# Scores of the first token block in a block-attention layer: one TensorE matmul over the keys' high and low parts side by side, and a VectorE add

## The chip, the cores and the metric

The kernel runs on one core of a Trainium2 chip. The metric is the device time of one execution in microseconds (us), taken as the median of several runs. Five engines matter: TensorE (PE in the rows, its weight loads PEld), VectorE (DVE), ScalarE (ACT), GpSimd (POOL) and the queue that issues the transfers (SP).

## What is computed

One attention layer of a decoder, 256 tokens of 1024 channels, 16 heads of 64, and a final RMSNorm. With 256 tokens and blocks of 256 keys there is only the token's own block, so the attention is causal softmax with a linear distance penalty:

```python
h = rms_norm(x, norm_g)
q, k, v, gate = split(h @ w_in, 4)                   # 1024 x 4096
s = (q . k) * 64**-0.5 - slope[head] * (t - pos)     # -inf where pos > t
o = softmax(s) @ v                                   # per head
x = x + (o * silu(gate)) @ w_out
out = rms_norm(x, final_norm_g)
```

All is float32. The kernel reaches that accuracy by splitting each operand into a high part (rounded to the matmul's input format) and a low part (the rest), and summing three products: high by high, high by low, low by high.

## The kernel before, in words

The 256 tokens are two token blocks of 128 (`m = 0`, `m = 1`). Heads are handled in eight pairs `p`: a pair's q and k lie transposed on the 128 partitions, 64 for each of its two heads (`a = 0, 1`), 256 tokens wide.

The body of the kernel is a long stream of TensorE matmuls for the input projection (column parts in the order of `PARTS`: v, q, k, gate and so on) and then for the output projection (`outmm`, one weight piece per `k`; for the last four `k` one output column group after the other). Each weight piece of 128 x 1024 is loaded by a transfer, rounded by ScalarE (`split_hi`, tile `whi`) and subtracted by VectorE (`split_lo`, tile `wlo`, line 251). The attention of each pair is a Python generator, a fiber, whose steps are emitted between the projection's matmuls. A planner (`Plan`) keeps a running estimate of TensorE's position and of the backlog of ScalarE and VectorE; a fiber's next step is emitted when the planned TensorE time has reached the time at which its input is planned to be ready (`yield`, `poll`, `until`). The result is one fixed order of instructions for each engine; the chip then works each engine's list in order.

A pair's steps are:

- `fiber_evac` multiplies a projection's PSUM bank by the row scale into `z` (line 497), ScalarE rounds it to the high part and VectorE subtracts (line 510) for the low part. The two parts of q and of k are two tiles each.
- `scores(p)`, called for an even `p`, does pairs `p` and `p + 1` together, in four PSUM banks, one for each head. For `m = 1` each head has a result of 128 x 256 in columns 0 to 255 of its bank; for `m = 0` the causal part is only 128 x 128, in columns 256 to 383. For each there are three matmuls, and the two heads of a pair work on different halves of the rows at the same time. There are four such score stages.
- `fiber_pair` then has VectorE add the bias (distance penalty and mask) to each result, read from PSUM, with the row's minimum of the negative as a by-product (line 380), ScalarE the exponential with the row sum, VectorE the reciprocal and the scaling (lines 390 to 403), TensorE the transposes of `pr` (line 111), ScalarE and VectorE their split (`pth`, `ptl`, line 426), TensorE the product with the values, ScalarE a copy (`cs`), VectorE two adds (`og`, line 458), the gate (line 462), ScalarE the rounding (`oh`) and VectorE the rest (`ol`, line 467). `oh` and `ol` of pair `p` are the operands of the output projection's piece `k = p`.

The score bank goes back to the pool after the `m = 0` step of its head (`give(bs[a], d)`).

Of the kernel before, what the change touches and what calls it, by code (L numbers as in the profile page):

```python
# [9 lines left out]
F32R = mybir.dt.float32r  # L10
# [3 lines left out]
P = 128  # L14
S = 256
# [72 lines left out]
def trunk(ctx: ExitStack, tc, laid, fin_g, out):  # L88
    nc = tc.nc
    plan = Plan()  # L90
# [32 lines left out]
    def dve(n, dep, rate=0.96, extra=0):  # L123
        return plan.op("dve", 66 + extra + n / rate, dep)
# [166 lines left out]
    qs, ks = {}, {}  # L291
# [32 lines left out]
    def scores(p):  # L324


        while not all(u in at_k and u in at_q for u in (p, p + 1)):
            yield poll()
        yield max(t[u] for t in (at_k, at_q) for u in (p, p + 1))
        while stage["s"] < p:  # L330
            yield poll()
        while True:
            b0 = take(keep[0] + 3)
            if b0 is not None:
                break
            yield poll()
        both = [b0] + [take_now() for _ in range(3)]
        plan.pe += SWITCH
        for u in (p, p + 1):
            of_pair[u] = both[2 * (u - p):2 * (u - p) + 2], {}  # L340
        for m, c in ((1, slice(0, S)), (0, slice(S, S + P))):
            for u in (p, p + 1):
                bs, at_s = of_pair[u]
                (qh, ql), (kh, kl) = qs[u], ks[u]
                for jj, (q, k) in enumerate(((qh, kh), (qh, kl), (ql, kh))):
                    for a in range(2):
                        rr = slice(a * DH, (a + 1) * DH)
                        nc.tensor.matmul(bs[a]["t"][:, c], q[rr, m * P:(m + 1) * P], k[rr, 0:c.stop - c.start],  # L348
                                         start=jj == 0, stop=jj == 2)
                    at_s[m] = plan.mm(c.stop - c.start)  # L350
        plan.pe += SWITCH
        stage["s"] = p + 2
        yield 0

    def fiber_pair(p):
        if p % 2 == 0:
            yield from scores(p)
        while stage["s"] <= p:
            yield poll()
        bs, at_s = of_pair.pop(p)  # L360
        while stage["t"] < p - NPR + 1:
            yield poll()
        st = sp.tile([P, 2, P + S], F32, name="st")
        pr = sp.tile([P, 2, P + S], F32, name="pr")
        mx = sm.tile([P, 4], F32, name="mx")
        rs = sm.tile([P, 4], F32, name="rs")
        ri = sm.tile([P, 4], F32, name="ri")
        r = at_s[0]
        yield 0
        for m in (1, 0):  # L370
            n = (m + 1) * P
            for a in range(2):
                yield r - 250
                while plan.t["act"] > plan.pe + BACK or plan.t["dve"] > plan.pe + BACK:
                    yield poll()
                c0, c1 = (0, P) if m == 0 else (P, P + S)
                bt = bias[:, 2 * p + a, P:S] if m == 0 else bias[:, 2 * p + a, :]
                cc = 2 * m + a
                ps = bs[a]["t"][:, 0:S] if m else bs[a]["t"][:, S:S + P]
                nc.vector.tensor_tensor_reduce(st[:, a, c0:c1], ps, bt, scale=-1.0, scalar=BIG,  # L380
                                               op0=ALU.add, op1=ALU.min, accum_out=mx[:, cc:cc + 1])
                d = dve(n, r, extra=8)
                yield d - 150
                e = act(pr[:, a, c0:c1], st[:, a, c0:c1], AF.Exp, n, d, False, scale=-1.0, bias=mx[:, cc:cc + 1],
                        accum=rs[:, cc:cc + 1])
                if m == 0:
                    give(bs[a], d)
        stage["e"] += 1
        yield e - 400
        nc.vector.tensor_scalar(rs, rs, 2.0, None, op0=ALU.mult)  # L390
        dve(4, e)
        yield plan.t["dve"] - 50
        nc.vector.reciprocal(ri, rs)
        d = d_ri = dve(4, e, extra=157)
        for a in range(2):
            for m in range(NM):
                c0, c1 = (0, P) if m == 0 else (P, P + S)
                cc = 2 * m + a
                o = pr[:, a, c0:c1]
                if plan.t["act"] + NORM < plan.t["dve"]:  # L400
                    d = max(d, act(o, o, AF.Copy, c1 - c0, d_ri, False, scale=ri[:, cc:cc + 1]))
                else:
                    nc.vector.tensor_scalar(o, o, ri[:, cc:cc + 1], None, op0=ALU.mult)
                    d = max(d, dve(c1 - c0, 0, rate=1.92, extra=62))
        d0 = d
        yield d0
        while stage["t"] < p or stage["v"] < p - NPT + 1:
            yield poll()
        hi = ptp.tile([P, 2, 3, P], F32R, name="pth")
        lo = ptp.tile([P, 2, 3, P], F32R, name="ptl")  # L410
        for a in range(2):
            while True:
                b = take(keep[0])
                if b is not None:
                    break
                yield poll()
            for jj in range(3):
                r = tr(b["t"][:, jj * P:(jj + 1) * P], pr[:, a, jj * P:(jj + 1) * P], d0)
                if a == 1 and jj == 2:
                    stage["t"] = p + 1  # L420
                yield 0
            pv = b["t"][:, :3 * P].rearrange("p (a n) -> p a n", a=3)
            yield r - 200
            e = act(hi[:, a], pv, AF.Copy, 3 * P, r, True)
            yield e - 200
            nc.vector.tensor_sub(lo[:, a], pv, f32(hi[:, a]))  # L426
            d = dve(3 * P, e)
            give(b, d)
        while nv[p // 4] < NM:
            yield poll()  # L430
        yield max(d, at_v[p // 4])
        while stage["v"] < p or p not in at_g:
            yield poll()
        while True:
            b = take(keep[0])
            if b is not None:
                break
            yield poll()
        po = b["t"].rearrange("p (a n) -> p a n", a=2)

        for a in range(2):
            w = [vv[m][:, 2 * p + a].rearrange("p t n -> p (t n)") for m in range(NM)]
            for jj, u in enumerate((hi, lo)):
                mm(po[:, a, :], w[0], u[:, a, 0:2, :], jj == 0, False, S)
            yield 0
            for jj, u in enumerate((hi, lo)):
                r = mm(po[:, a, P:S], w[1], u[:, a, 2, :], False, jj == 1, P)
            if a == 1:
                stage["v"] = p + 1
            yield 0  # L450
        yield r - 300
        cs = csp.tile([DH, 2, S], F32, name="cs")
        e = act(cs, po[DH:P], AF.Copy, 2 * S, r, True)
        yield e - 200
        og = ogp.tile([P, S], F32, name="og")
        for a in range(2):
            rr = slice(a * DH, (a + 1) * DH)
            nc.vector.tensor_add(og[rr, :], po[0:DH, a, :], cs[:, a, :])  # L458
            d = dve(S, e)
        give(b, d)  # L460
        yield max(d, at_g[p]) - 200
        nc.vector.tensor_mul(og, og, sg[:, p, :])
        d = dve(S, max(d, at_g[p]))
        yield d - 200
        e = act(oh[:, p, :], og, AF.Copy, S, d, False)
        yield e - 200
        nc.vector.tensor_sub(ol[:, p, :], og, f32(oh[:, p, :]))
        at_o[p] = dve(S, e)
# [6 lines left out]
    def fiber_evac(kind, j, f, b, r):  # L475
        ps = b["t"][:, :S]
        p = 2 * j + f
# [25 lines left out]
        yield d - 100  # L503
        if kind != "g":
            pool = qp if kind == "q" else khp
            hi = pool.tile([P, S], F32R, name=f"{kind}h")
            lo = pool.tile([P, S], F32R, name=f"{kind}l")
            e = act(hi, z, AF.Copy, S, d, False)
            yield e - 100
            nc.vector.tensor_sub(lo, z, f32(hi))  # L510
            (qs if kind == "q" else ks)[p] = (hi, lo)
            (at_q if kind == "q" else at_k)[p] = dve(S, e)
        else:
            e = act(sg[:, p, :], z, AF.Tanh, S, d, False, scale=0.5)
            yield e - 100
            nc.vector.scalar_tensor_tensor(sg[:, p, :], sg[:, p, :], 1.0, z, op0=ALU.add, op1=ALU.mult)
            at_g[p] = dve(S, e)

    with tc.manual_schedule():
# [132 lines left out]
        for kind, j in PARTS[1:]:  # L652
# [4 lines left out]
            for k in range(NK):  # L657
# [5 lines left out]
                for f in range(2):  # L663
                    fs = slice(f * P, (f + 1) * P)
                    for jj, (xx, ww) in enumerate(((xh, whi), (xl, whi), (xh, wlo))):
                        if kind == "v":
                            o, a, b = acc[f]["t"], xx[k][:, fs], ww[i][:, kk * w:(kk + 1) * w]
                        else:
                            o, a, b = acc[f]["t"][:, :S], ww[i][:, kk * w + f * P:kk * w + (f + 1) * P], xx[k]
# [33 lines left out]
        for m in range(NM):  # L703
# [4 lines left out]
            for u, (c0, c1) in enumerate(GROUPS[m]):  # L708
                c = slice(c0, c1)
# [63 lines left out]
```

## Time and profile before

| what | value |
|---|---|
| median of 3 runs | 146.40 us (146.39 to 146.41) |
| profiled execution | 146.18 us, of which the span from the first to the last instruction is 144.4 us |
| TensorE busy | 137.2 us (95% of the span), 1009 matmuls |
| VectorE busy | 119.5 us (83%), 291 instructions |
| ScalarE busy | 92.1 us (64%), 197 instructions |
| granted TensorE clock, mean | 0.99 of full speed |

A row of a timeline gives start, duration, engine, line, operation, output and inputs, the number of instructions merged, and in brackets how long the engine stood idle before it and what released it. Matmuls are pipelined: the row's duration of a matmul holds its latency, and its cost to the stream is read from start to start. "x2" at a score matmul is the two heads of a pair, which start together.

### The profile page before, as it was taken

Reading aid. Unit: us, or ns where it says so; the run is one execution under the profiler, and the core shown is the slowest. Engines: PE = TensorE matmul, PEld = TensorE weight load, DVE = VectorE, ACT = ScalarE, POOL = GpSimd, SP = SyncE. Lnnn points to the kernel's source line nnn. Section 1 sums busy time; section 2 is a strip of 40 time slices with the busy share of each in tenths; the row PEclk is TensorE's granted clock in tenths of the full one; section 3 lists DMA queues with packets and bytes.
Section 4 is the critical chain, followed back from the end, with each engine's and each line's share of the span. In section 5 each row is a group of like instructions: output and inputs, shape, how many; then the busy total and the mean of one; then the engine's idle time right before and its main releaser. Section 6 shows DMA issues by size and latency. Waiting matters only on the chain.

```text
span 144.4 us, 2760 instructions
## 1 busy us (share of the span) xinstructions
PE 137.2 (95%) x1009; PEld 126.0 (87%) x1009; DVE 119.5 (83%) x291; ACT 92.1 (64%) x197; POOL 13.6 (9%) x29
## 2 busy tenths in 40 slices
PE   7999999999999999999999999999999999999930
PEld 5588999999999999999988889999999888868830
DVE  0999399978877999999899699886869996975870
ACT  3698979657779476967293987426595855812330
POOL 7891140000000000000000000000000000000210
PEclk9999999999999999999999999999999999999995
DMA  5999998687015147454536215566614044000123
GB/s 150 350 393 409 414 405 320 201 291 257 22 49 188 58 145 232 137 178 180 194 110 205 82 47 184 204 241 215 239 42 150 0 145 145 0 0 5 39 108 145
DMA packets 8078, 24.83 MB, mean 172 GB/s; under 512 B 896, under 2 KB 1408, under 8 KB 8064
## 3 DMA queue, kind: packets, MB, share of 16 engines
q1 hardware_dynamic: 7632, 23.73, 46.3%
q10 hardware_dynamic: 432, 0.92, 1.7%
q8 instruction: 8, 0.13, 0.4%
q14 instruction: 6, 0.05, 0.1%
HBM read 23.60 MB, written 1.05 MB: 171 GB/s over the span
## 4 chain that ended last, share of the span: by engine, by line
PE 84%; issue 4%; ACT 3%; DVE 3%; DMA 2%; POOL 1%; POOLq 0%
PE bank L107 76%; PE bank L348 4%; PE bank L111 4%; DMA w<-in_laid 2%; ACT whi L118 1%; DVE xl L251 1%; ACT xh L118 1%; POOL fr L726 1%; DVE og L458 1%; DVE bias L717 1%; ACT oh L118 1%; ACT bias L728 1%; POOLq L769 0%; DVE x L715 0%; ACT cs L118 0%
## 5 line engine op out<-in xcount | busy, mean ns | idle before, releaser
L107 PE MATMUL bank<-xh,wlo 128*128 128x256 f32 x192 | 55.2, 288 | 0.0
L107 PE MATMUL bank<-xl,whi 128*128 128x256 f32 x192 | 55.2, 288 | 0.0
L107 PE MATMUL bank<-xh,whi 128*128 128x256 f32 x192 | 55.0, 287 | 0.0
L251 DVE TENSOR_TENSOR wlo<-w,whi 128x1024 fp32r<-128x1024 f32 (+1 forms) x43 | 48.8, 1141 | 6.6 <-ACT whi L118 6.6
L118 ACT ACTIVATE whi<-w 128x1024 fp32r<-128x1024 f32 (+1 forms) x43 | 41.9, 976 | 14.3 <-PE bank L107 7.6
L107 PEld LDWEIGHTS bank<-xl,whi 128*128 128x128 f32 x192 | 36.2, 189 | 0.2
L107 PEld LDWEIGHTS bank<-xh,wlo 128*128 128x128 f32 x192 | 36.2, 189 | 0.2
L107 PEld LDWEIGHTS bank<-xh,whi 128*128 128x128 f32 x192 | 36.2, 189 | 0.1
L118 ACT ACTIVATE pr<-st,mx 128x256 f32<-128x256 f32 (+1 forms) x32 | 14.2, 444 | 7.4 <-DVE mx L380 7.4
L107 PE MATMUL bank<-whi,ol 128*128 128x512 f32 (+1 forms) x35 | 12.8, 364 | 0.0
L726 POOL TENSOR_TENSOR fr<-fms,mhalf 128x1 f32<-128x1 f32 x2 | 1.6, 797 | 117.8 <-DVE fms L717 117.8
L107 PE MATMUL bank<-whi,oh 128*128 128x512 f32 (+1 forms) x35 | 12.6, 361 | 0.0
L107 PE MATMUL bank<-wlo,oh 128*128 128x512 f32 (+1 forms) x35 | 12.6, 359 | 0.0
L111 PE MATMUL bank<-ident,pr 128*128 128x128 f32 x48 | 12.1, 272 | 0.0
L107 PE MATMUL bank<-whi,xh 128*128 128x512 f32 x32 | 11.7, 407 | 0.2 <-ACT whi L118 0.2
L107 PE MATMUL bank<-wlo,xh 128*128 128x512 f32 x32 | 11.6, 403 | 0.0
L107 PE MATMUL bank<-whi,xl 128*128 128x512 f32 x32 | 11.5, 398 | 0.0
L497 DVE TENSOR_TENSOR z<-bank,rows 128x256 f32<-128x256 f32 x24 | 9.5, 419 | 2.3 <-PE bank L107 2.3
L380 DVE CUSTOM_DVE_ANT_0 st<-bank,bias 128x256 f32<-128x256 f32 (+1 forms) x32 | 9.8, 350 | 0.3 <-PE bank L348 0.3
L118 ACT ACTIVATE pth<-bank 128x384 fp32r<-128x384 f32 x16 | 7.8, 489 | 2.7 <-PE bank L111 2.4
L426 DVE TENSOR_TENSOR ptl<-bank,pth 128x384 fp32r<-128x384 f32 x16 | 8.6, 551 | 0.5 <-ACT pth L118 0.5
L107 PE MATMUL bank<-ptl,vv 128*128 128x256 f32 (+1 forms) x32 | 8.9, 279 | 0.0
(81 smaller groups left out, 209.8 us busy)
## 6 DMA issues: line engine op xcount, KB each, us to landing
w<-in_laid SPq DMA_DIRECT2D x36, 512.0 KB, 3.5
w<-in_laid SPq DMA_DIRECT2D x7, 256.0 KB, 4.9
x<-in_laid SPq DMA_DIRECT2D x2, 512.0 KB, 6.8
head<-in_laid SPq DMA_DIRECT2D x3, 256.0 KB, 5.1
out<-bias SPq DMA_DIRECT2D x2, 320.0 KB, 2.3
gf<-in_fin_g ACTq DMA_DIRECT2D x1, 512.0 KB, 5.5
out<-bias SPq DMA_DIRECT2D x2, 192.0 KB, 1.9
w<-in_laid ACTq DMA_DIRECT2D x1, 256.0 KB, 3.1
```

The lines of the kernel that those rows point to most:

```text
L107: nc.tensor.matmul(o, a, b, start=start, stop=stop)
L111: nc.tensor.transpose(o, a, ident)
L118: nc.scalar.activation(o, i, fn, scale=scale, **kw)
L251: nc.vector.tensor_sub(wlo[i][:, c], w32[i][:, c], f32(whi[i][:, c]))
L348: nc.tensor.matmul(bs[a]["t"][:, c], q[rr, m * P:(m + 1) * P], k[rr, 0:c.stop - c.start], start=jj == 0, stop=jj == 2)
L380: nc.vector.tensor_tensor_reduce(st[:, a, c0:c1], ps, bt, scale=-1.0, scalar=BIG, op0=ALU.add, op1=ALU.min, accum_out=mx[:, cc:cc + 1])
L426: nc.vector.tensor_sub(lo[:, a], pv, f32(hi[:, a]))
L458: nc.vector.tensor_add(og[rr, :], po[0:DH, a, :], cs[:, a, :])
L497: nc.vector.tensor_mul(z, ps, rows8 if kind == "q" else rows)
L717: nc.vector.tensor_tensor_reduce(sq[:, :c1 - c0], y[:, c], y[:, c], scale=1.0 / D, scalar=ms[:, u - 1:u], op0=ALU.mult, op1=ALU.add, accum ...
L726: nc.gpsimd.tensor_tensor(r, ms[:, ns - 1:ns], mhalf, op=ALU.pow)
L728: nc.scalar.activation(z[:, 0:CW], z[:, 0:CW], AF.Copy, scale=r)
```

## The change

For `m = 0` the three matmuls per head become two. The first has the high part of q as stationary operand and the high and the low part of k side by side as moving operand (2 x 128 columns); its result is 128 x 256, the high-by-high product in columns 256 to 383 and the high-by-low product in columns 384 to 511 of the head's bank. The second adds low q by high k to the first half. The two halves are added afterwards: VectorE adds the second half and the bias into `st`, and the instruction of line 380 takes `st` in place of the bias. For this the two parts of k (and of q) become two halves of one tile. `m = 1` keeps its three matmuls. The planner is told of the two matmuls (`plan.mm(n * len(ts))`) and of the add (`dve(n, r)`).

```diff
-                (qh, ql), (kh, kl) = qs[u], ks[u]
-                for jj, (q, k) in enumerate(((qh, kh), (qh, kl), (ql, kh))):
+                (qh, ql), kt = qs[u], ks[u]
+                n = c.stop - c.start
+                terms = ((qh, (0, 1)), (ql, (0,))) if m == 0 else ((qh, (0,)), (qh, (1,)), (ql, (0,)))
+                for jj, (q, ts) in enumerate(terms):
                     for a in range(2):
                         rr = slice(a * DH, (a + 1) * DH)
-                        nc.tensor.matmul(bs[a]["t"][:, c], q[rr, m * P:(m + 1) * P], k[rr, 0:c.stop - c.start],
-                                         start=jj == 0, stop=jj == 2)
-                    at_s[m] = plan.mm(c.stop - c.start)
+                        o = bs[a]["t"][:, c.start:c.start + n * len(ts)]
+                        o = o.rearrange("p (t n) -> p t n", n=n)
+                        nc.tensor.matmul(o, q[rr, m * P:(m + 1) * P], kt[rr, ts[0]:ts[-1] + 1, 0:n],
+                                         start=jj == 0, stop=jj == len(terms) - 1, skip_group_check=True)
+                    at_s[m] = plan.mm(n * len(ts))
@@
+                if m == 0:
+                    nc.vector.tensor_add(st[:, a, c0:c1], bs[a]["t"][:, S + P:S + 2 * P], bt)
+                    bt = st[:, a, c0:c1]
+                    dve(n, r)
                 nc.vector.tensor_tensor_reduce(st[:, a, c0:c1], ps, bt, scale=-1.0, scalar=BIG,
                                                op0=ALU.add, op1=ALU.min, accum_out=mx[:, cc:cc + 1])
@@
-            hi = pool.tile([P, S], F32R, name=f"{kind}h")
-            lo = pool.tile([P, S], F32R, name=f"{kind}l")
+            both = pool.tile([P, 2, S], F32R, name=kind)
+            hi, lo = both[:, 0], both[:, 1]
@@
-            (qs if kind == "q" else ks)[p] = (hi, lo)
+            (qs if kind == "q" else ks)[p] = (hi, lo) if kind == "q" else both
```

## Rows read from the trace of the kernel before

**Rows 1.** The page: busy time of the engines, share of the span, instructions.
```profile
PE 137.2 (95%) x1009; PEld 126.0 (87%) x1009; DVE 119.5 (83%) x291; ACT 92.1 (64%) x197; POOL 13.6 (9%) x29
```

**Rows 2.** The two longest waits of the weight loads of the projections (columns: who waited for whom, us in total, times, longest).
```profile
PEld bank L107 <- ACT whi L118: 0.9, 1, 0.9
PEld bank L107 <- ACT oh L118: 0.6, 1, 0.6
```

**Rows 3.** The chain of work that ended last, in order of time: the first and the last of the four score stages on it, which have the same length (start, us, engine, line, matmuls).
```profile
31.80 1.53 PE bank L348 x24
...
101.12 1.53 PE bank L348 x24
```

**Rows 4.** TensorE's timeline around the first score stage: the last step of `m = 1`, the first three and the last of the six steps of `m = 0`, and the projection's matmul that follows.
```profile
32.42 0.30 PE L348 MATMUL bank<-kh,ql 64*128 64x256 f32 x2
32.54 0.24 PE L348 MATMUL bank<-kh,qh 64*128 64x128 f32 x2
32.60 0.29 PE L348 MATMUL bank<-kl,qh 64*128 64x128 f32 x2
32.71 0.29 PE L348 MATMUL bank<-kh,ql 64*128 64x128 f32 x2
...
33.05 0.29 PE L348 MATMUL bank<-kh,ql 64*128 64x128 f32 x2
33.27 0.38 PE L107 MATMUL bank<-xh,wlo 128*128 128x256 f32 x1
```

**Rows 5.** Two of the weight loads of the same steps.
```profile
32.65 0.21 PEld L348 LDWEIGHTS bank<-kh,ql 64*128 64x128 f32 x2
32.76 0.21 PEld L348 LDWEIGHTS bank<-kh,qh 64*128 64x128 f32 x2
```

**Rows 6.** VectorE's groups by line and shape (instructions, busy us, mean ns of one): adds from PSUM of 256 and 384 columns, and the bias step of 128 columns.
```profile
L497 DVE TENSOR_TENSOR z<-bank,rows 128x256 f32<-128x256 f32 x24 | 9.5, 419 | 2.3 <-PE bank L107 2.3
L426 DVE TENSOR_TENSOR ptl<-bank,pth 128x384 fp32r<-128x384 f32 x16 | 8.6, 551 | 0.5 <-ACT pth L118 0.5
L380 DVE CUSTOM_DVE_ANT_0 st<-bank,bias 128x128 f32<-128x128 f32 x16 | 4.4, 282 | 0.0
```

**Rows 7.** VectorE's timeline after the last score stage, with the first (103.87) and the last (109.89) of its four bias steps of `m = 0`, and each instruction ahead of which VectorE stood idle for over 0.2 us.
```profile
103.87 0.29 DVE L380 CUSTOM_DVE_ANT_0 st<-bank,bias 128x128 f32<-128x128 f32 x1
...
104.54 0.42 DVE L497 TENSOR_TENSOR z<-bank,rows 128x256 f32<-128x256 f32 x1 [0.37 <-PE bank L107]
...
106.46 0.43 DVE L516 SCALAR_TENSOR_TENSOR head<-head,z 128x256 f32<-128x256 f32 x1 [0.27 <-ACT head L118]
107.79 1.23 DVE L251 TENSOR_TENSOR wlo<-w,whi 128x1024 fp32r<-128x1024 f32 x1 [0.91 <-ACT whi L118]
...
109.89 0.28 DVE L380 CUSTOM_DVE_ANT_0 st<-bank,bias 128x128 f32<-128x128 f32 x1
```

**Rows 8.** Two dependent instructions of VectorE, one behind the other, for pair 2 (reciprocal, scaling of `pr`).
```profile
60.34 0.18 DVE L393 RECIPROCAL ri<-rs 128x4 f32<-128x4 f32 x1
60.56 1.01 DVE L403 TENSOR_SCALAR pr<-pr,ri 128x128 f32<-128x128 f32 x4
```

**Rows 9.** Busy time of each engine (PE, PEld, DVE, ACT, POOL, each with its instructions; then the granted clock, the transfers' share and GB/s) in four stretches: score stages 1 and 2, each with what follows up to the first transposes of its pairs, stage 4 with what follows it, and the stretch behind that.
```profile
31.70:41.10 9.40, 9.40 (x91) 9.30 (x91) 7.78 (x32) 6.57 (x23) 0.00 (x0) 1.00 0.40 137
53.00:62.50 9.50, 9.50 (x93) 9.43 (x92) 9.16 (x32) 6.96 (x21) 0.00 (x0) 1.00 0.52 167
101.00:107.80 6.80, 6.80 (x69) 6.68 (x69) 4.84 (x20) 5.13 (x18) 0.00 (x0) 1.00 0.40 149
107.80:121.70 13.90, 13.90 (x96) 12.51 (x96) 12.74 (x32) 9.27 (x17) 0.00 (x0) 1.00 0.34 112
```

**Rows 10.** VectorE's timeline in the last part of the kernel: the splits of the transposes of the last two pairs, and what stands around them.
```profile
116.92 1.05 DVE L426 TENSOR_TENSOR ptl<-bank,pth 128x384 fp32r<-128x384 f32 x2
...
119.49 1.21 DVE L251 TENSOR_TENSOR wlo<-w,whi 128x1024 fp32r<-128x1024 f32 x1
121.76 0.85 DVE L458 TENSOR_TENSOR og<-bank,cs 64x256 f32<-64x256 f32 x2 [1.06 <-ACT cs L118]
122.64 0.56 DVE L426 TENSOR_TENSOR ptl<-bank,pth 128x384 fp32r<-128x384 f32 x1
```

**Rows 11.** TensorE's timeline: the first transpose of pair 2, the first matmul with the values for pair 6 (119.37) and for pair 7 (123.44), and the place where the output projection comes to piece 7.
```profile
62.18 0.27 PE L111 MATMUL bank<-ident,pr 128*128 128x128 f32 x1
...
119.37 0.28 PE L107 MATMUL bank<-pth,vv 128*128 128x256 f32 x1
...
123.44 0.28 PE L107 MATMUL bank<-pth,vv 128*128 128x256 f32 x1
...
128.59 0.39 PE L107 MATMUL bank<-whi,ol 128*128 128x512 f32 x1
129.13 0.50 PE L107 MATMUL bank<-xh,oh 128*128 128x512 f32 x1
```

**Rows 12.** The chain of work that ended last, its part from the values of pair 7 to piece 7 of the output projection.
```profile
125.57 0.60 ACT cs L118
...
127.07 1.23 DVE xl L251
128.66 0.43 ACT oh L118
...
129.13 3.77 PE bank L107 x15
```

## The prediction

> **What bounds the kernel now.** I began with the busy times: TensorE is busy for 95% of the span and VectorE for 83% [rows 1]. An average does not say which of them sets the end, so next I read who waited for whom. The longest waits of the projections' weight loads are one for ScalarE's `whi`, 0.9 us, and one for `oh`, 0.6 us [rows 2]; the first is that for the first pieces of the kernel, the second the one that the chain at the end goes through. From the first score stage to 128.59 us no other engine made a hole in TensorE's list. So there TensorE's own work sets the time, and a microsecond taken out of it is a microsecond, as long as the other engines keep up with a TensorE that runs earlier. The chain that ended last agrees: it runs along TensorE, all four score stages lie on it, of 1.53 us each [rows 3], and it leaves TensorE only near the end, for the last pair's `cs`, `og`, gate and `oh` [rows 12]. There TensorE stands: from 128.59 to 129.13 is 0.54 us start to start, where 15 matmuls took 3.77 us, 0.25 each, so about 0.29 us is waiting [rows 11, 12].
>
> So there are two questions: how much shorter a score stage gets, and whether VectorE, which gets more work, falls behind far enough to be met at the end.
>
> **TensorE's part.** The steps of `m = 0` have only 128 moving columns, and yet one follows another at 0.11 us: 32.60 to 32.71, and 32.60 to 33.05 for four steps, which is 0.1125 each. A step of `m = 1`, of 256 columns, takes 0.12 (32.42 to 32.54) [rows 4]. So halving the columns saves almost nothing. The weight loads of these steps stand at the same distance, 32.65 to 32.76 [rows 5]: every step brings a new stationary operand, and that sets the pace. The change replaces three loads per pair by two. Three steps of 0.11 become one of 0.12 and one of 0.11: 0.33 less 0.23 is 0.10 us for each pair, two pairs in a stage, four stages: 8 x 0.10 = 0.80 us. Bounds: the shortest distance in the rows is 0.06 (32.54 to 32.60, behind a 256-column step whose length hides a load) [rows 4]. If the dropped step were worth only that, 8 x (0.06 - 0.01) = 0.40 us; if it were worth a 256-column step, 8 x 0.12 = 0.96. I take 0.80, since four of the five distances between these steps are of that kind. That the two heads of a pair work side by side, and the 0.22 us from the last score step to the next projection matmul (33.05 to 33.27) [rows 4], stay as they are. The moving operand is now two runs of 128 columns with a gap of 128 between them. No row shows such an operand at full clock; I price it at nothing within the bound above, because the result is still one run of 256.
>
> A rule of the Trainium skill speaks against this gain. The page "TensorE: Matmul & The Clock Gate", section "Wait — 56ns, not 53.3ns?", has warm matmuls follow each other at columns / 2.4 GHz plus about 2.5 ns, which is 55.6 ns for 128 columns. By that rule the three steps would be 3 x 56 = 168 ns and the two 109 + 56 = 165 ns, an estimate, and merging would save nothing. The trace disagrees for these steps, with 112 ns; the same page, section "LDWEIGHTS (loading the stationary operand)", has a load of 128 columns take 128 / 1.2 = 107 ns, which is near the distance of the rows.
>
> **VectorE's part.** Sixteen adds of 128 columns, one operand in PSUM, come in; two per pair. The trace has no such add. An add from PSUM takes 419 ns at 256 columns and 551 at 384, 132 per 128 columns; one step further down is 287 ns. The bias step of the same 128 columns from the same bank takes 282 [rows 6]. The line 380 instruction behind each add needs its result, so the two cannot overlap: between dependent instructions the rows show a gap of 0.04 us (60.34 + 0.18 to 60.56) [rows 8]. I take 0.29 + 0.03 = 0.32 us each, 1.28 per stage, 5.1 in all. Bounds: 0.28, the bias step alone, and 0.42 + 0.04 = 0.46, the 256-column add; 4.5 to 7.4 us in all. No instruction of VectorE goes, so a gain there is excluded.
>
> What hides them is VectorE's idle time and the distance that the planner keeps. After stage 1 VectorE is idle for 9.40 - 7.78 = 1.62 us, more than 1.28. After stage 2 only for 9.50 - 9.16 = 0.34 us [rows 9]. There 0.94 us go into delay. The planner knows of part: its cost of an add is 66 + 128 / 0.96 = 199 ns, so it places what comes later by 4 x 0.20, and only 4 x 0.12 = 0.48 us come unannounced. Pair 2's `pr` is ready at 60.56 + 1.01 = 61.57 [rows 8] and its first transpose starts at 62.18 [rows 11]; 0.61 us are there, so TensorE is not held. If this cover were gone, the excess would be TensorE's loss at once, since its list is in order: queued behind a transpose is the whole projection. Late next would be the weight pieces' `wlo`, which stand behind in VectorE's list.
>
> After stage 4 there is no later stage to recover in, so I go through it in steps. VectorE stands idle for 0.37, 0.27 and 0.91 us between the first bias step of `m = 0` and 107.79, in all 1.55 us. Three of the four adds fall there (0.96 us); the fourth belongs to the step at 109.89 [rows 7], in a stretch where VectorE works for 12.74 of 13.90 us [rows 9], and pushes what follows by 0.32. TensorE is 0.80 us earlier by then. If the stretch starts as much earlier, VectorE is 0.32 us later against TensorE; if its start does not move at all, 1.12 us. At the end of the stretch the pair 6 splits are done at 116.92 + 1.05 = 117.97 [rows 10], and TensorE uses them at 119.37 [rows 11]: 1.40 us of distance, more than either. From there the last pairs follow TensorE: at 121.76 VectorE has been idle for 1.06 us, waiting for `cs`, which waits for those matmuls; the split of pair 7, which is behind `cs` in the list, is done at 122.64 + 0.56 = 123.20 [rows 10] for a use at 123.44 [rows 11]. So the chain of the last pair should start earlier with TensorE, and the wait of 0.29 us should stay about as it is.
>
> The planner takes something back, since it places the steps of a fiber by its own costs: VectorE's backlog in the plan is larger and TensorE's position earlier, so the last pair can land later among the output projection's matmuls. At worst it gives back the whole 0.80; at best nothing. Only the fourth add's 0.20 us falls into a stretch without idle time, so I take 0.15.
>
> The longer hold of a score bank (0.64 us for its pair) and the single tile for the two parts of q and k I cost at nothing: ScalarE and VectorE write the two halves one after the other as before, and the next use of a bank lies behind some microseconds of projection. If a bank is missing, a fiber's step moves, which is within the 0.80.
>
> **The sum.** The profiled execution took 146.18 us. 146.18 - 0.80 + 0.15 = 145.53. The median is 0.22 above that execution, so 145.7 us. Less than 0.2% (0.29 us) cannot be told from no change here.
>
> **The rivals.**
> - The order comes out better. VectorE's split of the last weight piece, 1.23 us, whose result lies in `xl`, stands between the last pair's adds and its gate (127.07) [rows 12]; if the new order puts it elsewhere, the 0.29 us wait at the end goes too. 145.75 - 0.15 - 0.29 gives 145.3. For it: the order near the end hangs on small differences of the plan. Against: nothing aims at it. Chance 0.12.
> - The gain is given back at the end: the last pair lands later in the plan by what TensorE gained, 0.5 to 0.8 us, and the wait for `oh` grows by that. 146.1 to 146.6, around 146.4. For it: the wait is there already [rows 2]. Chance 0.14.
> - The change does not shorten TensorE, because a two-run moving operand or the column count sets the pace, as the rule above has it: 146.4 us. Against it: 0.1125 us for a step of 128 [rows 4]. Chance 0.04.
> - Slower: VectorE sets the last pair. If all four adds of stage 4 are on the path (4 x 0.32 = 1.28 us), while the stage starts only three stages' gain earlier (0.60 us), `oh` of pair 7 is 0.68 us later than now, and with it all that follows: 147.1 us. This decides from the point where VectorE's lag against TensorE is over the 1.40 us of pair 6. For it: VectorE's full stretch of 13.9 us, and the dear end of the add (4 x 0.46 = 1.84 us) would carry it there. Against: 1.55 us of idle time before that stretch and 1.06 behind it. Chance 0.20, 146.7 to 147.4.
>
> **How the numbers follow.** The forecast has 0.50, from 145.4 to 146.05, the price of TensorE's steps and the planner's share being its width. Faster by over 0.2%: 0.50 + 0.12 = 0.62. Within 0.2%: 0.14 + 0.04 = 0.18. Slower: 0.20. Both signs hold much, so the range is 145.0 to 147.0: it leaves out the luckiest orders below and less than half of the slower case above.
>
> **What would show it.** A score stage in the chain should take 1.53 - 0.20 = 1.33 us, with 20 instead of 24 score matmuls, 993 matmuls in all (1009 [rows 1] less 16). The adds should last about 0.29 us, sixteen of them, and VectorE's busy time rise by some 16 x 0.29 = 4.6 us. The transposes and the matmuls with the values should still show no wait for VectorE. The last wait for `oh` should be near 0.3 us. I am wrong if the stages do not shrink (pace set otherwise), if the weight loads show new waits for `pr`, `ptl` or `wlo` (VectorE met), or if the wait for `oh` grows by the better part of 0.8 us.

## The result, and the profile after

The changed kernel takes 145.66 us, median of 19 runs, beside 146.53 us of the kernel before on the same chips. The ratio is 0.9937, with a 95% interval of 0.9919 to 0.9956: 0.9 us faster, between 0.6 and 1.2. The forecast was 145.7 us, faster.

Single runs spread over more than this, those of the changed kernel from 145.0 to 146.9 and those of the kernel before from 146.15 to 147.70. The profiled execution of the changed kernel took 145.95 us, in the upper half of its runs, and that of before 146.18 us, near the low end of its own. So the two spans, 144.1 and 144.4 us, show only 0.3 us of the gain. Part of the spread arises at the start, which is told at the end; the comparisons below therefore also run from the first score matmul to the last matmul of the kernel, which leaves the start out. Even so two traces of one kernel, the changed one, differ by 0.15 us (105.98 and 105.83 in the table).

The page of the changed kernel, busy times, to stand beside [rows 1]:

```profile
PE 136.7 (95%) x993; PEld 125.7 (87%) x993; DVE 122.9 (85%) x306; ACT 93.4 (65%) x198; POOL 13.6 (9%) x29
```

Sixteen matmuls are gone. VectorE has sixteen adds more and one scaling of `pr` less, which the planner's new order gives to ScalarE (198 instructions in place of 197). The chain of work that ended last has the four score stages, as in [rows 3]:

```profile
32.04 1.32 PE bank L353 x20
...
54.16 1.32 PE bank L353 x20
...
78.82 1.31 PE bank L353 x20
...
100.09 1.33 PE bank L353 x20
```

Each stage has 20 matmuls in place of 24 and takes 1.32 us in place of 1.53. Adding up the start-to-start times of all score matmuls gives 5.28 us after and 6.12 before, 0.84 us less.

VectorE's groups of the bias step (to compare with [rows 6]), and two rows of its timeline after stage 2, an add and the instruction that needs it:

```profile
L389 DVE CUSTOM_DVE_ANT_0 st<-bank,st 128x128 f32<-128x128 f32 x16 | 4.7, 292 | 0.6
L386 DVE TENSOR_TENSOR st<-bank,bias 128x128 f32<-128x128 f32 x16 | 4.6, 285 | 0.0
```
```profile
59.42 0.28 DVE L386 TENSOR_TENSOR st<-bank,bias 128x128 f32<-128x128 f32 x1
59.74 0.29 DVE L389 CUSTOM_DVE_ANT_0 st<-bank,st 128x128 f32<-128x128 f32 x1
```

The add lasts 285 ns and holds VectorE for 0.32 us, since the next instruction starts only behind its end. The place where the output projection comes to piece 7 (TensorE's timeline, to compare with [rows 11]):

```profile
128.12 0.40 PE L107 MATMUL bank<-whi,ol 128*128 128x512 f32 x1
128.81 0.51 PE L107 MATMUL bank<-xh,oh 128*128 128x512 f32 x1 [0.30 <-ACT oh L118]
```

Start to start this is 0.69 us, where it was 0.54: the wait for the last pair's `oh` has grown by 0.15 us.

### The profile page after: what moved, and what is told of

Its sections match the earlier page's. It is cut to its first block, busy times and chain, and to the rows that moved or that the text cites. A ratio compares the mean times of both kernels' runs of the same rounds, so it can differ in the third digit from the quotient of the medians.

```text
span 144.1 us, 2750 instructions
## 1 busy us (share of the span) xinstructions
PE 136.7 (95%) x993; PEld 125.7 (87%) x993; DVE 122.9 (85%) x306; ACT 93.4 (65%) x198; POOL 13.6 (9%) x29
## 4 chain that ended last, share of the span: by engine, by line
PE 81%; DVE 8%; issue 3%; DMA 2%; ACT 1%; POOL 1%; POOLq 0%
PE bank L107 74%; PE bank L353 4%; PE bank L111 3%; DVE wlo L251 2%; DMA head<-in_laid 2%; DVE ptl L435 1%; DVE og L467 1%; DVE xl L251 1%; ACT pth L118 1%; POOL fr L735 1%; DVE pr L412 1%; DVE bias L726 1%; ACT bias L737 1%; POOLq L778 0%; DVE x L724 0%
## 5 line engine op out<-in xcount | busy, mean ns | idle before, releaser
L220 POOL TENSOR_SCALAR bias<-dist 128x256 f32<-128x256 f32 x16 | 8.6, 537 | 1.0
```

Source lines behind the costliest of these rows:

```text
L220: nc.gpsimd.tensor_scalar(bias[:, h, :], dist, slope, 0.0, op0=ALU.mult, op1=ALU.add)
```

## The experiments

My theory at this point: TensorE is shorter by the load of one stationary operand per pair, VectorE's adds are hidden, and the planner's new order gives 0.15 us back at `oh`. Rivals: the moving columns set the pace of a score step; the new order makes the gain; the adds stand on the path and eat part of it; VectorE is bound at the end.

For every kernel the table gives the median of its runs, the ratio to before with its interval, the profiled execution's first score matmul and last matmul, and the difference of the two. Ratios are to the kernel before on the same chip, where its median was 146.54 us beside e1, e3, e4 and e5, 146.35 beside e2, e6, e7 and e8, and 146.53 beside e9 and e10; between groups the ratios are to be compared, not the medians.

| kernel | median us | ratio (95%) | first score matmul | last matmul | difference |
|---|---|---|---|---|---|
| before | 146.53 | 1 | 31.73 | 138.27 | 106.54 |
| changed | 145.66 | 0.9937 (0.9919 to 0.9956) | 31.97 | 137.96 | 105.98 |
| changed, again (e10) | 145.45 | 0.9938 (0.9919 to 0.9957) | 31.72 | 137.55 | 105.83 |
| e1, no adds | 145.60 | 0.9947 (0.9924 to 0.9970) | 31.82 | 137.70 | 105.88 |
| e2, adds alone | 146.74 | 1.0028 (1.0002 to 1.0053) | 32.83 | 139.60 | 106.77 |
| e3, narrow first matmul | 145.63 | 0.9939 (0.9920 to 0.9959) | 32.44 | 138.19 | 105.75 |
| e4, change in the order of before | 145.59 | 0.9938 (0.9913 to 0.9962) | 32.07 | 137.96 | 105.89 |
| e5, order of the change alone | 146.41 | 0.9986 (0.9967 to 1.0004) | 31.74 | 138.44 | 106.70 |
| e6, piece 7 late | 145.86 | 0.9969 (0.9955 to 0.9983) | 31.82 | 137.11 | 105.29 |
| e7, two adds | 146.64 | 1.0005 (0.9985 to 1.0026) | 32.02 | 138.52 | 106.49 |
| e8, four adds | 156.90 | 1.0692 (1.0657 to 1.0728) | 31.75 | 148.81 | 117.05 |
| e9, piece 7 late, other norm order | 145.68 | 0.9950 (0.9932 to 0.9968) | 32.05 | 137.34 | 105.29 |

**What sets the pace of a score step (e3).**

```diff
-                        o = bs[a]["t"][:, c.start:c.start + n * len(ts)]
-                        o = o.rearrange("p (t n) -> p t n", n=n)
-                        nc.tensor.matmul(o, q[rr, m * P:(m + 1) * P], kt[rr, ts[0]:ts[-1] + 1, 0:n],
+                        o = bs[a]["t"][:, c.start:c.start + n]
+                        nc.tensor.matmul(o, q[rr, m * P:(m + 1) * P], kt[rr, ts[0], 0:n],
@@
-                    nc.vector.tensor_add(st[:, a, c0:c1], bs[a]["t"][:, S + P:S + 2 * P], bt)
+                    nc.vector.tensor_add(st[:, a, c0:c1], ps, bt)
```

> The changed kernel with a first matmul of 128 moving columns instead of 2 x 128 (high q by low k is left out, the add takes the first half a second time); two matmuls per head and the order stay. My theory, that a step of the score stage is set by the load of its stationary operand: a stage of 1.29 to 1.33 us in place of 1.33, and the whole the same as the changed kernel within 0.2 us. Rival, that the moving columns set the pace: each of the eight first steps takes about half as long, 0.4 us less in all, 145.2.

The score stages in its chain of work, first and last:

```profile
32.51 1.30 PE bank L352 x20
...
100.26 1.31 PE bank L352 x20
```

Taking the low half of the moving operand away shortens a stage by about 0.02 us. The start-to-start times of all score matmuls add up to 5.22 us, against 5.28 and 5.30 in the two traces of the changed kernel; if the columns set the pace, 0.4 us would have gone. The ratio is that of the changed kernel. So 256 columns cost next to what 128 do here. A fixed cost of 0.11 us for each matmul does not fit either, since one step follows another at 0.06 us in [rows 4]. What is left is the stationary operands, three in the kernel before and two now; that it is their loads rests on the distance of the loads in [rows 5], for no run drops a load and keeps its matmul.

**Is it the order (e5, e4).** e5 keeps the three matmuls and has no add, and lets the planner book the changed kernel's costs:

```diff
-                    at_s[m] = plan.mm(c.stop - c.start)
+                    if m == 1:
+                        at_s[m] = plan.mm(S)
+                    elif jj != 1:
+                        at_s[m] = plan.mm(S if jj == 0 else P)
@@
+                if m == 0:
+                    dve(n, r)
                 nc.vector.tensor_tensor_reduce(st[:, a, c0:c1], ps, bt, scale=-1.0, scalar=BIG,
```

> The kernel before, its three matmuls and no add, but in the order that the planner gives the changed kernel. My theory, that the gain is TensorE's dropped steps: 0.84 us slower than the changed kernel, 146.4, the same as before within 0.2 us, its wait for oh at the end below that of the changed kernel. Rival, that the new order makes the gain: 145.6, like the changed kernel.

Its first score stage in the chain, and TensorE's timeline at piece 7:

```profile
31.81 1.53 PE bank L348 x24
```
```profile
128.62 0.40 PE L107 MATMUL bank<-whi,ol 128*128 128x512 f32 x1
129.31 0.50 PE L107 MATMUL bank<-xh,oh 128*128 128x512 f32 x1 [0.30 <-ACT oh L118]
```

The new order alone gains nothing that can be measured; in the traces it loses 0.16 us (106.70 against 106.54), about as much as two traces of one kernel differ. One thing I expected is wrong: the wait for `oh` is not below that of the changed kernel but the same, 0.69 us start to start. e4 is the reverse, the whole change in the order of before:

```diff
-                    at_s[m] = plan.mm(n * len(ts))
+                    for _ in ts:
+                        at_s[m] = plan.mm(n)
@@
-                    dve(n, r)
```

> The whole change, but the planner books the score stage and VectorE as before the change, so every engine keeps the order of the kernel before. My theory: the score stages give 0.84 us as in the changed kernel; VectorE's 1.28 us per stage now come wholly unannounced, which after stage 2 is about 0.3 us over the distance to the transposes, and the wait for oh grows by 0 to 0.6. Between 145.7 and 146.3. Rival, that the gain is the new order's and not the matmuls': the same as before, 146.5.

```profile
128.28 0.39 PE L107 MATMUL bank<-whi,ol 128*128 128x512 f32 x1
128.82 0.50 PE L107 MATMUL bank<-xh,oh 128*128 128x512 f32 x1 [0.15 <-ACT oh L118]
```

It has the whole gain, a little more than I had put down (145.59, below my 145.7 to 146.3), and its wait is 0.54 us, that of before, although VectorE has its adds unannounced. So the size of the wait goes with the order, not with the adds. In the whole time the order cannot be told: the changed kernel has the same ratio as e4.

What the order does to the wait can be read off the last pair. These are the first matmul with its values, the split of the last weight piece (`xl`) and the pair's own steps up to `oh`, from three engines' timelines of the changed kernel; those of before are in [rows 11, 12]:

```profile
124.86 0.28 PE L107 MATMUL bank<-pth,vv 128*128 128x256 f32 x1
125.87 1.22 DVE L251 TENSOR_TENSOR xl<-w,xh 128x1024 fp32r<-128x1024 f32 x1
126.34 0.60 ACT L118 ACTIVATE cs<-bank 64x512 f32<-64x512 f32 x1 [1.19 <-PE bank L107]
127.01 0.84 DVE L467 TENSOR_TENSOR og<-bank,cs 64x256 f32<-64x256 f32 x2
127.88 0.43 DVE L471 TENSOR_TENSOR og<-og,head 128x256 f32<-128x256 f32 x1
128.34 0.42 ACT L118 ACTIVATE oh<-og 128x256 fp32r<-128x256 f32 x1 [1.41 <-DVE og L471]
```

Three shifts add up. From the first matmul with the values to the last matmul ahead of `oh`'s use there were 5.15 us (123.44 to 128.59) and are now 3.26 (124.86 to 128.12), 1.89 less. From that first matmul to the end of `cs` it takes 0.65 less (2.08 in place of 2.73). From the end of `cs` to the start of `oh` it takes 1.09 less (1.40 in place of 2.49), since `xl` no longer stands between the adds and the gate. 1.89 less 0.65 less 1.09 leaves 0.15 us. The traces of e1, e3, e5, e7, e8 and e10, which keep this order, show the same 3.26 us, those of e2 and e4 the 5.15 of before.

**What the adds cost (e1, e2).** e1 leaves the adds out of the changed kernel; e2 puts them into the kernel before.

```diff
e1, against the changed kernel
-                    nc.vector.tensor_add(st[:, a, c0:c1], bs[a]["t"][:, S + P:S + 2 * P], bt)
-                    bt = st[:, a, c0:c1]
e2, against the kernel before
+                if m == 0:
+                    nc.vector.tensor_add(st[:, a, c0:c1], ps, bt)
+                    bt = st[:, a, c0:c1]
```

> The changed kernel without VectorE's sixteen adds (the products of high q by low k are then left out of the scores of the first token block); the planner still books them, so every engine's order is that of the changed kernel. My theory, that VectorE's idle time hides the adds: within 0.2 us of the changed kernel, about 145.6, with a last wait for oh near the 0.44 us that the changed kernel shows, at most 0.2 us less. Rival, that the adds stand on the path and eat part of a larger gain of TensorE: 0.3 us or more faster than the changed kernel, and the wait for oh shrinks to nothing.

> The kernel before with its three matmuls and its order, and sixteen adds of VectorE ahead of the bias steps of the first token block (each adds the same scores once more, so these scores count twice). My theory, that VectorE's idle time and the distance to TensorE's uses hide an add of 0.32 us: 146.5, the same as before within 0.25 us, the wait for oh as before (0.29 us). Rival, that VectorE is near enough to the bound for 1.28 us per stage to show: 0.5 us or more slower, with new waits of weight loads for pr, ptl or wlo.

TensorE's timeline of e1 at piece 7:

```profile
127.86 0.40 PE L107 MATMUL bank<-whi,ol 128*128 128x512 f32 x1
128.56 0.50 PE L107 MATMUL bank<-xh,oh 128*128 128x512 f32 x1 [0.29 <-ACT oh L118]
```

Without the adds the changed kernel is no faster: 0.9947 against 0.9937, and 105.88 us against 105.98 and 105.83. The wait for `oh` stays at 0.70. In the kernel before they cost 0.28% (0.02 to 0.53), some 0.4 us, a little over my 0.25, and 0.23 us by the traces (106.77 against 106.54), and no wait for `pr` or `ptl` appears. So the adds are hidden in the changed kernel, and close to it in the one before, where 0.23 us is little more than the 0.15 between two traces of one kernel.

**How much room is left (e7, e8).** Each add is done twice, and four times:

```diff
+                    for _ in range(2):          # 4 in e8
                         nc.vector.tensor_add(st[:, a, c0:c1], bs[a]["t"][:, S + P:S + 2 * P], bt)
```

> The changed kernel with each of the sixteen adds done twice, in the same order of instructions. My theory: some 0.2 to 0.3 us more for each, 0.9 to 1.2 us per stage, unannounced, while the distance of TensorE's uses from VectorE's results is 0.6 to 1.4 us: 0 to 0.4 us slower than the changed kernel, 145.7 to 146.1. Rival, that the adds are already on the path: slower by four adds at the last stage at the least, 0.9 us or more, 146.6.

> The same with each add done four times, which is 2.5 to 3.5 us more of VectorE per stage. My theory: more than any distance in the trace, so TensorE has to wait for pr, ptl and wlo, and at the last stage it cannot be made up: 1.5 to 4 us slower than the changed kernel, 147 to 150. Rival, that VectorE is far from the bound everywhere: within 0.5 us of the changed kernel.

The second add takes the whole gain back: 1.0005 against 0.9937. I had expected at most 0.4 us. By the ratios it is 1.0 us, the rival's number, and by the traces 0.5 us (106.49 against 105.98). But it is not lost at the last stage, as the rival had it. VectorE's scaling of pair 2 and TensorE's first transpose of it, first in the changed kernel, then in e7:

```profile
64.08 0.74 DVE L412 TENSOR_SCALAR pr<-pr,ri 128x128 f32<-128x128 f32 x3
65.00 0.27 PE L111 MATMUL bank<-ident,pr 128*128 128x128 f32 x1
```
```profile
65.20 0.74 DVE L413 TENSOR_SCALAR pr<-pr,ri 128x128 f32<-128x128 f32 x3
65.54 0.33 PE L111 MATMUL bank<-ident,pr 128*128 128x128 f32 x1 [0.31 <-DVE pr L413]
```

The scaling is 1.12 us later, and TensorE stands still for 0.31 us until it has the first part of it. The transpose waits for the first of the scalings only, not for all: it starts at 65.54, when the three last until 65.94. Counted from the first score matmul, the transpose starts 0.49 us later than in the changed kernel (65.54 less 32.02, against 65.00 less 31.97), and the last matmul 0.51. So nearly the whole loss of the trace has arisen by here. Of the four stretches of [rows 9] this is the one with VectorE's least idle time, and the wait of `oh` at the end is unchanged in e7 (0.69). With four adds the waits of the weight loads are:

```profile
PEld bank L111 <- DVE pr L413: 7.6, 3, 2.9
PEld bank L107 <- ACT oh L118: 1.4, 1, 1.4
```

It costs 11 us, far more than the 1.5 to 4 us that I put down: three stages wait for `pr`, up to 2.9 us each, and what comes behind them in TensorE's list waits too.

**Can the 0.15 us, and the rest of the wait, be had (e6, e9).** e6 puts piece 7 later for the first token block; e9 adds to it another order in the final norm of that block: both column groups are added first, the products with the norm's weights come last (its further lines are not shown).

```diff
e6
+            if m == 0:
+                for c0, c1 in GROUPS[m]:
+                    for k in range(NK - 4, NK - 1):
...
+                        outmm(k, m, c0, c1, accs[m, c0]["t"][:, :c1 - c0])
             for u, (c0, c1) in enumerate(GROUPS[m]):
...
-                for k in range(NK - 4, NK):
+                for k in range(NK - 4 if m else NK - 1, NK):
```

> The changed kernel with one edit in the output projection: for the first token block pieces 4 to 6 are done for both column groups before piece 7 is asked for, which puts some 2.1 us of matmuls between the last pair's values and its first use. My theory, that the wait of 0.44 us for oh in the changed kernel comes from where the last pair stands in TensorE's order, and that nothing else is met there: the wait is gone and the time falls by 0.3 to 0.45 us against the changed kernel, 145.3. Rival, that VectorE or ScalarE is behind there anyway, or the final norm sets the end: no gain, 145.66.

> The changed kernel with piece 7 of the output projection late for the first token block, as in the run before, and in the final norm of that block both column groups are added before VectorE turns to the sum of squares and the product with the norm's weights. My theory: with piece 7 late TensorE ends about 0.7 us earlier and VectorE's list in the final norm sets the end; the second column group's add then comes some 0.6 us earlier, and with it the end: 145.1 to 145.3. Rival, that VectorE's list is bound further on, by the second block's chain: no gain over the changed kernel, 145.7.

The wait is gone in both and TensorE ends 0.5 to 0.7 us earlier (105.29 against 105.83 and 105.98), but the time does not fall, as the rivals of both had it: 0.9969 and 0.9950, where the changed kernel has 0.9937. VectorE's timeline of the final norm, first of the changed kernel, then of e6:

```profile
132.62 0.69 DVE L724 TENSOR_TENSOR x<-bank,x 128x512 f32<-128x512 f32 x1 [1.16 <-PE bank L107]
...
135.69 0.69 DVE L724 TENSOR_TENSOR x<-bank,x 128x512 f32<-128x512 f32 x1
```
```profile
131.07 0.69 DVE L730 TENSOR_TENSOR x<-bank,x 128x512 f32<-128x512 f32 x1 [2.13 <-PE bank L107]
131.80 0.69 DVE L737 TENSOR_TENSOR bias<-x,gf 128x512 f32<-128x512 f32 x1
...
132.63 0.68 DVE L730 TENSOR_TENSOR x<-bank,x 128x512 f32<-128x512 f32 x1
...
135.69 0.68 DVE L730 TENSOR_TENSOR x<-bank,x 128x512 f32<-128x512 f32 x1
```

In e6 the first group's add comes later, because its piece 7 does (131.07; 129.82 in the changed kernel), so VectorE does the first group's work just when the second group's is ready, and starts the second (132.63) and the second token block (135.69) at the same times as in the changed kernel. e9 takes that work out of the way:

```profile
131.30 1.38 DVE L730 TENSOR_TENSOR x<-bank,x 128x512 f32<-128x512 f32 x2 [2.13 <-PE bank L107]
...
133.65 1.29 DVE L747 TENSOR_TENSOR bias<-x,gf 128x512 f32<-128x512 f32 x2
135.05 0.62 DVE L751 TENSOR_SCALAR bias<-bias,fr 128x384 f32<-128x384 f32 x2
135.58 0.68 DVE L730 TENSOR_TENSOR x<-bank,x 128x512 f32<-128x512 f32 x1
```

Now the two products (133.65, 1.29 us) stand in front of the second token block, which starts at 135.58, 0.11 us earlier than in the changed kernel. The span ends with it: at 144.06 us in the changed kernel and in e6, at 143.95 in e9. So once TensorE ends earlier, VectorE's list in the final norm sets the end. Neither version beats the changed kernel.

The changed kernel once more, on the chip of e9:

> The changed kernel itself once more, to stand beside the last kernel on the same chip: 145.66, 0.6% faster than before; from the first score matmul to the last matmul of the kernel 105.8 to 106.1 us, whatever the start does.

It gave 0.9938 and 105.83 us.

## Why the prediction was right, point by point

- **TensorE's steps, 0.80 us (0.40 to 0.96).** Measured 0.84. The price of a step was read right from the 0.11 us between the old steps and their loads [rows 4, 5], and e3 shows that the columns do not set it. That the load does is what the rows leave over, not what a run tested by itself. The Trainium skill's rule ("TensorE: Matmul & The Clock Gate", section "Wait — 56ns, not 53.3ns?"), 55.6 ns for 128 columns, would have had no gain; the traces disagree, since the columns are not what bounds these steps, which are 112 ns apart. The load time that the Trainium skill gives on the same page, section "LDWEIGHTS (loading the stationary operand)", 107 ns, is near the 112 ns of the rows. The moving operand in two runs, priced at nothing, cost nothing beyond the 0.02 us a stage by which e3 is shorter.
- **The adds, 0.32 us each.** Measured 285 ns and 0.32 us to the dependent start. The forecast of VectorE's busy time was too high: it rose by 3.4 us, not 4.6. Against e1, which has the same order without adds and 118.9 us, the adds are worth 4.0; the new order takes 0.7 us away (e5, that order without adds, has 118.8 against 119.5 before). What makes up the rest, 0.6 us, is not shown.
- **Their cover.** Hidden, as forecast (e1). That stage 2 is the tight place was right and e7 shows it. The distance there was mis-sized: I measured 0.61 us from the end of all four scalings of `pr` [rows 8, 11], while the transpose waits for the first alone. The first starts at 60.56 and such a scaling lasts 0.28 us, so the kernel before had 1.34 us. In the changed kernel 0.64 are left (64.08 and 0.28 to 65.00); the 1.12 us by which e7 is later exceed them by 0.48, which is about what its trace loses.
- **The last stage.** No wait of TensorE for VectorE between 107 and 123 us appeared. The distance at pair 6, 1.40 us in the kernel before, fell to 0.60, by the new order: the split ends at 118.66 and its use comes at 119.26, and e1, without adds, has the split wait for ScalarE's `pth` until 117.85. The rival that ends slower did not come. A second add per head takes the gain back, though at stage 2 (e7), and four make the kernel slower (e8).
- **The planner's share, 0.15 us.** The wait for `oh` grew by 0.15 us, and e5 and e4 show that the order did it. That the amount came out is luck: I took it from the fourth add's 0.20 us in the plan. What happened is that two of my rivals came together and nearly cancelled. The last pair's values land 1.89 us later against piece 7, and `xl` is out of the pair's way, which with the shorter way to `cs` gives 1.74 back. The sign "the last wait for `oh` should be near 0.3 us" was wrong: 0.29 and 0.15 make 0.44.
- **The sum.** In the first trace it is 106.54 to 105.98, 0.56 us: 0.84 less 0.15, less 0.13 spread over the projections' stream. In the second trace of the changed kernel it is 0.71, with nothing lost there. The medians give 0.9 (0.6 to 1.2). Where the 0.2 to 0.3 us between traces and medians come from is not shown; it is within the interval. The forecast gain, 0.65, stands at the low end of that interval. That the time came out to 0.1 us has some luck in it: I started from 146.40 us, the median of three runs, and the median of nineteen is 146.53.

## What to carry to other kernels

A matmul with few moving columns that brings its own stationary operand cost 0.11 us here with 128 columns and 0.12 with 256, so two products that share the stationary operand can go side by side for nearly the price of one; read the pace from the start-to-start times of the rows, not from the columns. What the merged result needs afterwards goes to another engine, and there the question is the stage with the least idle time, not the average: here one add per head was free and a second one took the gain back. Where a planner lays out the order anew, test the order by itself (e4, e5), and read what it did to the last pair before calling its share small. Before buying back a wait near the end, see what stands in the last engine's list behind it.

## What the runs showed that I had not expected

Part of the spread between runs is made at the start. Up to the first score stage the profiled kernels' work is the same, and the stage begins between 31.72 and 32.83 us. It is not all of it: the two traces of the changed kernel differ by 0.25 us there and by 0.15 from there to the last matmul. The latest start is e2. ScalarE's timeline, first of the kernel before, then of e2, at the third piece of x:

```profile
5.83 0.51 ACT L118 ACTIVATE xh<-head 128x256 fp32r<-128x256 f32 x1 [0.40 <-DMA head<-in_laid]
```
```profile
7.41 0.51 ACT L118 ACTIVATE xh<-head 128x256 fp32r<-128x256 f32 x1 [2.03 <-DMA head<-in_laid]
```

One early transfer landed later, ScalarE waited 2.03 us in place of 0.40, and TensorE's matmuls, elsewhere 0.23 us apart, have 0.93 us between two of them (7.79 to 8.72). The first score stage of e2 is 1.1 us later than that of before; some of the rest comes from two slow steps ahead of this, of 0.43 and 0.38 us. In e3 there are only slow steps: from 4.99 to 7.12 us its matmuls of 512 columns followed each other at 0.43 us, and its first score stage began at 32.44. The granted clock of that stretch reads 1.00, the upper level, as it does in the kernel before, so what makes them slow is open. Differences below 1 us between two single executions of this kernel say little unless the start is taken out.
